# One operand of VectorE's two-input instructions, and the later modulation sums, moved to PSUM

## The chip, the core and the metric

The kernel runs on one core of one Trainium2 chip. The metric is the device time of one execution in microseconds (us); the figure for a kernel is the median of its runs. Engines are named as in the profile: PE is TensorE, DVE is VectorE, ACT is ScalarE, POOL is GpSimd, SP is the queue that issues the DMAs. SBUF is the large on-chip memory, PSUM the small one into which TensorE writes, here eight banks of 128 lanes by 512 float32.

## The reference

One block of a diffusion transformer with a hybrid mixer, batch 1, 512 tokens and 256 context tokens, width 2048. All is float32.

```python
mod = silu(c) @ w_mod + b_mod; mod_c = silu(c_ctx) @ w_mod + b_mod     # six chunks of 2048 each
h_lat = rms_norm(x, nw[0]) * (1 + sc_m) + sh_m                         # the context likewise
p = concat([h_ctx, h_lat]) @ w_in                                      # 6176 columns: x, y, q, k, v, z, gates
# RG-LRU, 8 heads of 128: conv of 4 taps over x, sigmoid gates r and i, then in both directions
log_a = -8 * r * softplus(-lam); a = exp(log_a); u = sqrt(-expm1(2 * log_a)) * (i * x)
h_t = a_t * h_{t-1} + u_t
lru = (h_forward + h_backward) * gelu(y)
# gated delta rule, 8 heads of 128, both directions: conv of 4 taps and silu over q, k, v; q, k l2-normalised;
# per chunk a unit lower triangular solve, then a recurrence of a 128x128 state over the chunks
gdn = rms_norm(o_forward + o_backward) * silu(z)
x = x + g_m * rms_norm(concat([lru, gdn]) @ w_out, nw[1])
h = rms_norm(x, nw[2]) * (1 + sc_f) + sh_f
out = x + g_f * rms_norm(square(relu(h @ w_ff1)) @ w_ff2, nw[3])
```

## The kernel before

Every large product runs in split form: an operand is cast to a high part (ScalarE, line 67, `wh<-wr`), the rest is a low part (a subtraction in `tt`, line 61, on VectorE or GpSimd, `wl<-wr,wh`), and three products high-high, high-low, low-high are summed in a bank.

The work falls in three stages. First the modulation chunks 0 and 1 are made for both streams (lines 308 to 332), and the context is normalised, scaled and shifted by `to_fm` (line 241). Second comes the mixer: `run_tiles` goes through a fixed list of tiles of 128 columns of `w_in`, each of 16 k-steps of three products (lines 498 to 500) into one bank; its order is the string `ORD`. A tile's evacuation (`lru_x`, `lru_y`, `Group.evac`, `z_evac`) begins when its last product has been issued. Third are the output projection in two passes of two token tiles (`project`, `prep`, `m_evac`), and then the squared-relu MLP (lines 1452 to 1465).

Between the tiles stands background work. Each piece is a Python generator (`Task`): a group of instructions, then a `yield` with its VectorE and ScalarE cost in us and the number of slots to let pass. `slot` is called after a quarter of a 512-token tile; it adds 2.8 us of VectorE budget and 2.2 us of ScalarE budget and lets tasks run while the budget holds. `boundary` ties each engine's instructions to within one to three slots of their place in the program. All of this is decided when the program is built. Engines run their instructions in program order, and an instruction that waits holds what is queued behind it on its engine.

What the change touches:

- `stt` (line 64) and `tt` (line 61) are the helpers through which nearly all two-input VectorE instructions go, so their rows carry these two lines and are told apart by tile names: `pg` is an SBUF page of 128x512, `bk` a bank, `macc` a running sum, `ld` a loaded page, `c` and `btL` are per-lane scalars.
- `bank()` takes one of eight banks from a single pool, for tiles and background work alike.
- `taps` (lines 509 to 511): three multiply-adds of a convolution, shifted by -2, -1 and +1. `Group.evac` (line 764 on) copies the tile out of its bank (775), scales it (776), runs the taps, a tanh (782), a product, and for the last of a pair transposes the result on TensorE (`transp`, 238).
- `lru_ctx` and `lru_lat` (lines 557 to 644): gates through tanh, then exp, tanh, sqrt on ScalarE and products and scans on VectorE.
- `Group.run`: decay masks (841 to 843), the inversion of 32x32 diagonal blocks on VectorE in 31 steps of a product and a subtraction (lines 893 to 900), block doubling by small products, then the recurrence over tiles, in which one step asks for up to five banks.
- `modacc` (line 1119): for each of the chunks 2 to 5 and each quarter of its columns, 16 loaded pages of `w_mod` are multiplied by a per-lane scalar and added up in `macc`, which is then stored in HBM. Chunks 2 to 4 run as a task from the mixer on; chunk 5 runs in the MLP, ordered behind `after`. GpSimd clears `macc` first (1123), and it has one buffer.

Of the kernel before, what the change touches and what calls it, by code (L numbers as in the profile page):

```python
# [7 lines left out]
F32 = mybir.dt.float32  # L8
# [8 lines left out]
P = 128  # L17
# [14 lines left out]
def build(tc, A, out, stop=None, dump=None):  # L32
# [3 lines left out]
    with es:  # L36
# [113 lines left out]
        # silu(c), silu(c_ctx)  # L150
# [12 lines left out]
        sm = es.enter_context(tc.tile_pool(name="small", bufs=4))  # L163

        def rsqrt(x, w):
            """x: [P, w] f32 (>0), returns tile with x^-0.5"""
            y = sm.tile([P, 16], I32, tag="rq_y", name=nm("rqy"))[:, :w]
            t = sm.tile([P, 16], F32, tag="rq_t", name=nm("rqt"))[:, :w]
            V.tensor_scalar(out=y, in0=x.bitcast(I32), scalar1=-0.5, scalar2=MAGIC, op0=ALU.mult, op1=ALU.add)
            yf = y.bitcast(F32)  # L170
            for _ in range(3):
                stt(t, yf, -0.5, yf, ALU.mult, ALU.mult)
                tt(V, t, t, x, ALU.mult)
                stt(yf, t, 1.5, yf, ALU.add, ALU.mult)
            return yf

        def softplus(dst, x, w):
            """dst = log(1+exp(x)); tiles [P, w]"""
# [5 lines left out]
            tt(V, e, q, m, ALU.add)                      # -|x|  # L184
# [3 lines left out]
            tt(V, e, e, q, ALU.mult)                     # s = e/(2+e)  # L188
            tt(V, q, e, e, ALU.mult)                     # s^2
# [8 lines left out]
        def rnorm(parts):  # L198
            """parts: 4 aps [P, 512] of one token tile -> 1/rms column"""
# [6 lines left out]
        def rfin(acc):  # L206
            """sums of squares of four parts -> 1/rms column; the guess is negative, each step flips the sign"""
# [33 lines left out]
        def to_fm(src, hi, lo, sc4, sh4):  # L241
            """token-major page -> (x*sc+sh) transposed, split into hi/lo views [P, 4, 128]"""
# [3 lines left out]
            tt(V, v4(x), v4(b), sc4.unsqueeze(2).to_broadcast(sh), ALU.mult)  # L246
            tt(V, v4(x), v4(x), sh4.unsqueeze(2).to_broadcast(sh), ALU.add)
# [24 lines left out]
        scol = const([P, 2, 16], F32, "scol")     # nw0*(1+sc)  (lat, ctx)  # L272
# [3 lines left out]
        def hctx(f):  # L276
            """one of hi, lo of the context's 4 feature tiles: two parts of two"""
# [56 lines left out]
        hgb = const([P, 4, 8], F32, "hgb")            # half gate biases, (dir,gate),head  # L334
# [5 lines left out]
        sp2 = const([P, 2, 8], F32, "sp2")             # 2*softplus(-lam)  # L340
        sp4 = const([P, 2, 8], F32, "sp4")             # -4*softplus(-lam)
# [8 lines left out]
        mpar = const([P, 2], F32, "mpar")              # lane's row parity (block, row parity, unit)  # L350
# [37 lines left out]
        def slot(part=1):  # L388
            """background work that goes with a quarter of a tile's products"""
# [127 lines left out]
        gateD = dp.tile([16, P, 512], F32, name="gateD")     # gelu gates, then silu gates  # L517

        def lru_x(h, n):
            """evacuation of one x tile: conv, then the recurrence as a task"""  # L520
            w = [cvw[:, j, h:h + 1] for j in range(4)]

            def evac(pt):
                xr = page()[:, :n]
                xc = page()[:, :n]
                if n == LAT:
                    S.copy(xc.rearrange("p (c r) -> p c r", r=8), pt.rearrange("p (r c) -> p c r", c=64))
                else:
                    S.copy(xc, pt[:, :n])
# [27 lines left out]
        def lru_ctx(h, xr):  # L557
# [3 lines left out]
            th = []  # L561
            for g in range(2):
                b = bank()
                t = page()
# [5 lines left out]
                th.append(t)  # L570
            yield 0, 1.5, 0
            tr, ti = th
# [5 lines left out]
            S.activation(tr, tr, AF.Sqrt)  # L578
            tv = ti.rearrange("p (d n) -> p d n", d=2)
            stt(tv, tv, 1.0, xr.unsqueeze(1).to_broadcast([P, 2, n]), ALU.add, ALU.mult)  # L580
            yield 0.6, 2.6, H0
            stt(tr, a, 1.0, tr, ALU.add, ALU.mult)
            stt(ti, tr, 0.5, ti, ALU.mult, ALU.mult)
            yield 1.3, 0, 0
            V.tensor_tensor_scan(ti[:, :n], a[:, :n], ti[:, :n], 0.0, ALU.mult, ALU.add)
            V.tensor_copy(lst[:, h, 0:1], ti[:, n - 1:n])
            u1, a1 = ti[:, n:], a[:, n:]
            V.tensor_tensor_scan(u1[:, ::-1], a1[:, ::-1], u1[:, ::-1], 0.0, ALU.mult, ALU.add)
# [4 lines left out]
        def lru_lat(h, xr):  # L593
# [3 lines left out]
            for d in range(2):  # L597
                for g, th in enumerate((tr, ti)):
# [3 lines left out]
                    S.activation(t, b, AF.Tanh, bias=hgb[:, 2 * d + g, h:h + 1], scale=0.5)  # L602
                    th.append(t)
                yield 0, 1.2, 0
# [7 lines left out]
            for d in range(2):  # L612
                S.activation(tr[d], tr[d], AF.Sqrt)
                stt(ti[d], ti[d], 1.0, xr, ALU.add, ALU.mult)
            yield 1.3, 1.1, H0
            for d in range(2):
                stt(tr[d], a[d], 1.0, tr[d], ALU.add, ALU.mult)
                stt(ti[d], tr[d], 0.5, ti[d], ALU.mult, ALU.mult)
                yield 1.3, 0, 0
            while h not in ldone:  # L620
                yield 0, 0, H0
            for d in range(2):
                init = lst[:, h, d:d + 1]
                u, v = ti[d], a[d]
                if d == 0:
                    V.tensor_tensor_scan(u, v, u, init, ALU.mult, ALU.add)
                else:
                    V.tensor_tensor_scan(u[:, ::-1], v[:, ::-1], u[:, ::-1], init, ALU.mult, ALU.add)
            res = ti
            del tr, a  # L630
# [4 lines left out]
            yield 1.4, 0, 0  # L635
            tt(V, res[0], res[0], res[1], ALU.add)
            yield 0.6, 0, H0
# [8 lines left out]
        def lru_y(h):  # L646
            def evac(py):
                x, t = page(), page()
                S.copy(x, py)
                S.activation(t, py, AF.Square)  # L650
# [898 lines left out]
```

## Time and profile before

| | |
|---|---|
| median of 3 runs | 2912.62 us |
| lowest, highest | 2910.87, 2915.26 us |
| span of the profiled execution | 2909.7 us |
| PE, DVE, ACT, POOL busy | 2664.2, 1877.2, 1230.1, 699.8 us |
| mean granted TensorE clock | 0.965 |

The profile is one execution. A group's row gives line, engine, operation, what it writes and reads, shapes, count, busy time and the mean of one in ns, then the idle time of the engine in front of it and what ended it. A row of the waits gives who waited, for what, the sum in us, the number of waits and the longest. A row of the timeline begins with the start in us and the duration in us. The stage rows give the busy time and count for each engine, the granted clock, the DMA share and GB/s. Matmuls overlap in TensorE's pipeline, so a busy TensorE is not always at its peak.

### The profile page before, as it was taken

The page shows a single profiled execution, that of the slowest core. Times are in us where ns is not written, and L with a number is a line of the kernel's source. Part 1 is how long each engine was busy: PE and PEld are TensorE (multiplying, and loading weights), DVE is VectorE, ACT ScalarE, POOL GpSimd, SP SyncE. Part 2 cuts the span into 40 slices and gives each one's busy share as a digit, 9 for nine tenths or more (in the row PEclk, how much of TensorE's full clock was granted, in tenths as well). Part 3 has the DMA queues.
Part 4 walks back from the last instruction along what each step waited for, and adds up shares of the span by engine and source line. Part 5 has one row for each costly group of instructions (what it writes and reads, how often), then busy time and mean ns, then how long its engine had stood idle before and what let it go on. Part 6 is the DMA issues. An engine that isn't in the chain of part 4 may idle for free.

```text
span 2909.7 us, 39480 instructions
## 1 busy us (share of the span) xinstructions
PE 2664.2 (92%) x14189; PEld 2187.2 (75%) x14189; DVE 1877.2 (65%) x3288; ACT 1230.1 (42%) x2438; POOL 699.8 (24%) x586
## 2 busy tenths in 40 slices
PE   5788898888988987996899999999999999999998
PEld 1277697677876876875689887888888888888886
DVE  6988868989898879774679644443344443344446
ACT  4546476564536654453454222222222222222223
POOL 3555345443435445332620000000000000000002
PEclk8899899999999998998999999999999999999999
DMA  7754365555655655764578733233332333332335
GB/s 263 259 161 120 103 172 151 148 158 164 191 164 178 188 166 165 232 201 159 183 243 267 235 101 116 94 101 95 96 100 94 97 99 95 100 96 95 101 94 156
DMA packets 376631, 436.41 MB, mean 150 GB/s; under 512 B 22793, under 2 KB 213602, under 8 KB 376434
## 3 DMA queue, kind: packets, MB, share of 16 engines
q1 hardware_dynamic: 376434, 433.89, 48.0%
q8 instruction: 111, 1.82, 0.3%
q14 instruction: 86, 0.70, 0.1%
HBM read 402.35 MB, written 31.46 MB: 149 GB/s over the span
## 4 chain that ended last, share of the span: by engine, by line
PE 49%; DVE 2%; DMA 1%; issue 0%; ACT 0%; POOL 0%; SPq 0%; DVEq 0%; ACTq 0%; POOLq 0%
PE bk L1465 8%; PE bk L1464 8%; PE bk L1463 8%; PE bk L1453 7%; PE bk L1454 7%; PE bk L1452 7%; PE bk L1375 1%; PE bk L1374 1%; PE bk L1373 1%; PE bk L1424 1%; PE bk L1423 1%; PE bk L1422 1%; DMA wr<-in_w_ff 1%; DVE pg L61 0%; DVE wl L61 0%
## 5 line engine op out<-in xcount | busy, mean ns | idle before, releaser
L67 ACT CAST wh<-wr 128x512 fp32r<-128x512 f32 x952 | 587.3, 619 | 1224.7 <-PE bk L1453 444.3
L61 DVE TENSOR_TENSOR wl<-wr,wh 128x512 fp32r<-128x512 f32 x642 | 457.3, 714 | 774.4 <-ACT wh L67 652.7
L61 POOL TENSOR_TENSOR wl<-wr,wh 128x512 fp32r<-128x512 f32 (+1 forms) x310 | 438.3, 1419 | 594.8 <-ACT wh L67 551.2
L1463 PE MATMUL bk<-wh,pg 128*128 128x512 f32 x960 | 373.5, 389 | 0.0
L1464 PE MATMUL bk<-wh,pg 128*128 128x512 f32 x960 | 373.5, 389 | 0.0
L1465 PE MATMUL bk<-wl,pg 128*128 128x512 f32 x960 | 373.4, 389 | 0.0
L1452 PE MATMUL bk<-H2h,wh 128*128 128x512 f32 x896 | 349.0, 389 | 0.0
L1454 PE MATMUL bk<-H2h,wl 128*128 128x512 f32 x896 | 348.6, 389 | 0.0
L1453 PE MATMUL bk<-H2l,wh 128*128 128x512 f32 x896 | 348.5, 389 | 0.0
L498 PE MATMUL bk<-Hlh,wh 128*128 128x512 f32 (+1 forms) x784 | 322.1, 411 | 2.8 <-ACT wh L67 2.8
L500 PE MATMUL bk<-Hlh,wl 128*128 128x512 f32 (+1 forms) x784 | 315.2, 402 | 5.4 <-POOL wl L61 5.4
L499 PE MATMUL bk<-Hll,wh 128*128 128x512 f32 (+1 forms) x784 | 314.7, 401 | 0.0
L61 POOL TENSOR_TENSOR big<-big,pg 128x512 f32<-128x512 f32 x9 | 12.0, 1343 | 1244.1 <-ACT pg L1525 1244.1
L64 DVE SCALAR_TENSOR_TENSOR macc<-ld,silc,macc 128x512 f32<-128x512 f32 x256 | 229.2, 895 | 20.5 <-DMA ld<-in_w_mod 13.1
L1463 PEld LDWEIGHTS bk<-wh,pg 128*128 128x128 f32 x960 | 180.2, 188 | 37.5
L1464 PEld LDWEIGHTS bk<-wh,pg 128*128 128x128 f32 x960 | 180.2, 188 | 37.3
L1465 PEld LDWEIGHTS bk<-wl,pg 128*128 128x128 f32 x960 | 180.2, 188 | 37.2
L1452 PEld LDWEIGHTS bk<-H2h,wh 128*128 128x128 f32 x896 | 168.2, 188 | 35.2 <-issue 0.2
L1453 PEld LDWEIGHTS bk<-H2l,wh 128*128 128x128 f32 x896 | 168.2, 188 | 35.1 <-issue 0.2
L1454 PEld LDWEIGHTS bk<-H2h,wl 128*128 128x128 f32 x896 | 168.2, 188 | 34.7
L500 PEld LDWEIGHTS bk<-Hlh,wl 128*128 128x128 f32 (+1 forms) x784 | 151.0, 193 | 43.4 <-POOL wl L61 8.9
L498 PEld LDWEIGHTS bk<-Hlh,wh 128*128 128x128 f32 (+1 forms) x784 | 151.8, 194 | 34.6 <-ACT wh L67 3.7
(335 smaller groups left out, 4756.6 us busy)
## 6 DMA issues: line engine op xcount, KB each, us to landing
wr<-in_w_ff SPq DMA_DIRECT2D x272, 512.0 KB, 3.6
wr<-in_w_in SPq DMA_DIRECT2D x144, 512.0 KB, 4.0
ld<-in_w_mod SPq DMA_DIRECT2D x256, 256.0 KB, 3.3
mr<-in_w_mod SPq DMA_DIRECT2D x32, 1024.0 KB, 5.3
wr<-in_w_out SPq DMA_DIRECT2D x64, 512.0 KB, 4.7
pg<-vkD SPq DMA_DIRECT2D x88, 128.0 KB, 3.8
ld<-in_x SPq DMA_DIRECT2D x32, 256.0 KB, 5.1
vkD<-pg SPq DMA_DIRECT2D x24, 256.0 KB, 2.1
```

What stands on the lines that cost most here:

```text
L61: e.tensor_tensor(out=out, in0=a, in1=b, op=op)
L64: V.scalar_tensor_tensor(out=out, in0=a, scalar=s, in1=b, op0=op0, op1=op1)
L67: S.copy(hi, src)
L498: T.matmul(pt[:m, :n], wh, a, start=k == 0, stop=False)
L499: T.matmul(pt[:m, :n], wh, b, start=False, stop=False)
L500: T.matmul(pt[:m, :n], wl, a, start=False, stop=k == 15)
L1452: T.matmul(bk[c], w[kk][0][:, s_], hh, start=k == 0, stop=False)
L1453: T.matmul(bk[c], w[kk][0][:, s_], hl_, start=False, stop=False)
L1454: T.matmul(bk[c], w[kk][1][:, s_], hh, start=False, stop=k == 15)
L1463: T.matmul(o, ah, h, start=k == 0, stop=False)
L1464: T.matmul(o, al, h, start=False, stop=False)
L1465: T.matmul(o, ah, l, start=False, stop=k == 3)
```

## The change

Wherever a two-input VectorE instruction of the mixer read both inputs from SBUF, one is now taken from a bank where that could be had: the product's own bank is read in place of a copy, ScalarE writes its result into a bank, or VectorE computes in a bank in place. Instructions stay on their engines but for a memset that goes from GpSimd to VectorE. The running sums of `modacc` live in a bank for chunks 2 to 4 (`after is None`) and are copied to SBUF by ScalarE at the end; for chunk 5 they stay. Declared costs of some `yield`s change with it. The weight splits (`wl<-wr,wh`), small square-root arithmetic and the splits of the first modulation rows are as before. Comments were taken out, which is not shown. The core of the diff:

```diff
 def to_fm(src, hi, lo, sc4, sh4):
-            tt(V, v4(x), v4(b), sc4.unsqueeze(2).to_broadcast(sh), ALU.mult)
-            tt(V, v4(x), v4(x), sh4.unsqueeze(2).to_broadcast(sh), ALU.add)
+            tt(V, v4(b), v4(b), sc4.unsqueeze(2).to_broadcast(sh), ALU.mult)
+            tt(V, v4(x), v4(b), sh4.unsqueeze(2).to_broadcast(sh), ALU.add)
 lru_x:
-                xc = page()[:, :n]
                 if n == LAT:
+                    xc = bank()
                     S.copy(xc.rearrange("p (c r) -> p c r", r=8), pt.rearrange("p (r c) -> p c r", c=64))
                 else:
-                    S.copy(xc, pt[:, :n])
+                    xc = pt[:, :n]
 lru_ctx (lru_lat in the same way):
+            stt(ti.rearrange("p (d n) -> p d n", d=2), b.rearrange("p (d n) -> p d n", d=2), 1.0,
+                xr.unsqueeze(1).to_broadcast([P, 2, n]), ALU.add, ALU.mult)
...
-            S.activation(tr, tr, AF.Sqrt)
-            stt(tv, tv, 1.0, xr.unsqueeze(1).to_broadcast([P, 2, n]), ALU.add, ALU.mult)
-            yield 0.6, 2.6, H0
-            stt(tr, a, 1.0, tr, ALU.add, ALU.mult)
-            stt(ti, tr, 0.5, ti, ALU.mult, ALU.mult)
+            u = bank()
+            S.activation(u, tr, AF.Sqrt)
+            yield 0, 2.6, H0
+            stt(u, a, 1.0, u, ALU.add, ALU.mult)
+            stt(u, u, 0.5, ti, ALU.mult, ALU.mult)
 lru_lat:
-                    V.tensor_tensor_scan(u, v, u, init, ALU.mult, ALU.add)
+                    V.tensor_tensor_scan(ti[0], a[0], u, init, ALU.mult, ALU.add)
 lru_y:
-                S.copy(x, py)
-                S.activation(t, py, AF.Square)
-                V.tensor_scalar(out=t, in0=t, scalar1=0.044715, scalar2=1.0, op0=ALU.mult, op1=ALU.add)
-                tt(V, t, t, x, ALU.mult)
+                S.activation(t, py, AF.Square, scale=math.sqrt(0.044715))
+                stt(t, t, 1.0, py, ALU.add, ALU.mult)
...
-                stt(t, t, 1.0, x, ALU.add, ALU.mult)
+                stt(t, t, 1.0, py, ALU.add, ALU.mult)
 Group.evac:
-                    raw = page()[:, :n]
-                    S.copy(raw, pt[:, :n])
+                    raw = pt[:, :n]
                     S.activation(dst, raw, AF.Copy, scale=w[2])
                     taps(dst, raw, w, n)
-                    yield 1.7, 1, 0
+                    yield 1.7, 0.6, 0
...
-                    th = page()
+                    th = bank()
                     S.activation(th, cv, AF.Tanh, scale=0.5)
                     stt(cv, th, 1.0, cv, ALU.add, ALU.mult)
 Group.run:
-                        S.activation(dt, bD, AF.Exp)
+                        S.activation(bD, bD, AF.Exp)
-                            stt(v4(dt)[:, u, :], v4(dt)[:, u, :], gt["bt"][:, o + u:o + u + 1], mk, ALU.mult, ALU.mult)
+                            stt(v4(dt)[:, u, :], v4(bD)[:, u, :], gt["bt"][:, o + u:o + u + 1], mk, ALU.mult, ALU.mult)
...
-                Wt = page(shape=(P, 16, 32))
+                wf = bank()
+                Wt = wf.rearrange("p (j i) -> p j i", i=32)
-                G.memset(Wt, 0.0)
+                V.memset(wf, 0.0)
...
-                    S.activation(oT, b, AF.Copy, scale=gnh)
+                    stt(oT, b, gnh, sz[p], ALU.mult, ALU.mult)
-                    tt(V, self.oT[p], self.oT[p], sz[p], ALU.mult)
 z_evac:
-                S.copy(x, pz)
-                stt(sz, sz, 1.0, x, ALU.add, ALU.mult)
+                stt(sz, sz, 1.0, pz, ALU.add, ALU.mult)
 modacc:
-            acc = page(tag="macc", bufs=1)
+            acc = seed = page(tag="macc", bufs=1)
             G.memset(acc, 0.0)
             SP.dma_start(acc[0:1, :], A["b_mod"][:, col:col + 512])
+            if after is None:
+                acc = bank()
-                    stt(acc, q.pop(0), silc[:, k - 1:k], acc, ALU.mult, ALU.add)
+                    stt(acc, q.pop(0), silc[:, k - 1:k], seed if k == 1 else acc, ALU.mult, ALU.add)
-            SP.dma_start(accD[4 * (chunk - 2) + f], acc)
+            if after is None:
+                S.copy(seed, acc)
+            SP.dma_start(accD[4 * (chunk - 2) + f], seed)
 m_evac:
-                    x = m1[t][c]
-                    tt(V, x, x, bk[t], ALU.add)
+                    tt(V, x, m1[t][c], x, ALU.add)
```

More of the change, by code (lines that the diff above doesn't have):

```diff
@@ L560, in lru_ctx @@
             yield 0, 0.9, 2 * H0
-            th = []
+            tr, ti = page(), page()
             for g in range(2):
                 b = bank()
-                t = page()
+                t = b if g else tr
                 for d in range(2):
@@ L577, in lru_ctx @@
                 S.activation(tr[:, sl], tr[:, sl], AF.Tanh, bias=sp2[:, d, h:h + 1], scale=sp2[:, d, h:h + 1])
-            S.activation(tr, tr, AF.Sqrt)
-            tv = ti.rearrange("p (d n) -> p d n", d=2)
-            stt(tv, tv, 1.0, xr.unsqueeze(1).to_broadcast([P, 2, n]), ALU.add, ALU.mult)
-            yield 0.6, 2.6, H0
-            stt(tr, a, 1.0, tr, ALU.add, ALU.mult)
-            stt(ti, tr, 0.5, ti, ALU.mult, ALU.mult)
+            u = bank()
[3 more added lines that the diff above has]
+            stt(u, u, 0.5, ti, ALU.mult, ALU.mult)
             yield 1.3, 0, 0
-            V.tensor_tensor_scan(ti[:, :n], a[:, :n], ti[:, :n], 0.0, ALU.mult, ALU.add)
+            V.tensor_tensor_scan(ti[:, :n], a[:, :n], u[:, :n], 0.0, ALU.mult, ALU.add)
             V.tensor_copy(lst[:, h, 0:1], ti[:, n - 1:n])
-            u1, a1 = ti[:, n:], a[:, n:]
-            V.tensor_tensor_scan(u1[:, ::-1], a1[:, ::-1], u1[:, ::-1], 0.0, ALU.mult, ALU.add)
+            u1, a1, s1 = ti[:, n:], a[:, n:], u[:, n:]
+            V.tensor_tensor_scan(u1[:, ::-1], a1[:, ::-1], s1[:, ::-1], 0.0, ALU.mult, ALU.add)
             V.tensor_copy(lst[:, h, 1:2], u1[:, 0:1])
@@ L597, in lru_lat @@
             for d in range(2):
-                for g, th in enumerate((tr, ti)):
+                for g in range(2):
                     b = bank()
@@ L601, in lru_lat @@
                     t = page()
-                    S.activation(t, b, AF.Tanh, bias=hgb[:, 2 * d + g, h:h + 1], scale=0.5)
-                    th.append(t)
-                yield 0, 1.2, 0
+                    S.activation(b if g else t, b, AF.Tanh, bias=hgb[:, 2 * d + g, h:h + 1], scale=0.5)
+                    (tr, ti)[g].append(t)
+                stt(ti[d], b, 1.0, xr, ALU.add, ALU.mult)
+                yield 0.7, 1.2, 0
             del gate
@@ L611, in lru_lat @@
             yield 0, 3, 0
[L612 to L619, printed above, removed]
             while h not in ldone:
                 yield 0, 0, H0
+            us = []
             for d in range(2):
+                u = bank()
+                S.activation(u, tr[d], AF.Sqrt)
+                us.append(u)
+            yield 0, 1.1, H0
+            for d in range(2):
+                u = us[d]
+                stt(u, a[d], 1.0, u, ALU.add, ALU.mult)
+                stt(u, u, 0.5, ti[d], ALU.mult, ALU.mult)
                 init = lst[:, h, d:d + 1]
-                u, v = ti[d], a[d]
                 if d == 0:
-                    V.tensor_tensor_scan(u, v, u, init, ALU.mult, ALU.add)
+                    V.tensor_tensor_scan(ti[0], a[0], u, init, ALU.mult, ALU.add)
                 else:
-                    V.tensor_tensor_scan(u[:, ::-1], v[:, ::-1], u[:, ::-1], init, ALU.mult, ALU.add)
+                    V.tensor_tensor_scan(u[:, ::-1], a[1][:, ::-1], u[:, ::-1], init, ALU.mult, ALU.add)
+                    tt(V, ti[0], ti[0], u, ALU.add)
+                yield 2.7 + 0.7 * d, 0, 0
             res = ti
-            del tr, a
+            del tr, a, us, u
             while h not in gy:
@@ L634, in lru_lat @@
             SP.dma_start(t, gateD[h])
-            yield 1.4, 0, 0
-            tt(V, res[0], res[0], res[1], ALU.add)
-            yield 0.6, 0, H0
+            yield 0, 0, H0
             pr = res[1]
@@ L647, in evac @@
             def evac(py):
-                x, t = page(), page()
-                S.copy(x, py)
-                S.activation(t, py, AF.Square)
-                V.tensor_scalar(out=t, in0=t, scalar1=0.044715, scalar2=1.0, op0=ALU.mult, op1=ALU.add)
-                tt(V, t, t, x, ALU.mult)
-                yield 1, 1, H0
+                t = page()
+                S.activation(t, py, AF.Square, scale=math.sqrt(0.044715))
+                stt(t, t, 1.0, py, ALU.add, ALU.mult)
+                yield 0.7, 0.6, H0
                 S.activation(t, t, AF.Tanh, scale=math.sqrt(2.0 / math.pi))
-                stt(t, t, 1.0, x, ALU.add, ALU.mult)
+                stt(t, t, 1.0, py, ALU.add, ALU.mult)
                 yield 0.6, 0.5, H0
@@ L1076, in run @@
                     oT = page()
-                    S.activation(oT, b, AF.Copy, scale=gnh)
+                    stt(oT, b, gnh, sz[p], ALU.mult, ALU.mult)
                     self.oT.append(oT)
-                yield 0, 1.2, H0
-                for p in range(2):
-                    tt(V, self.oT[p], self.oT[p], sz[p], ALU.mult)
                 del sz
-                yield 1.2, 0, 0
+                yield 1.4, 0, 0
                 for p in range(2):
@@ L1093, in f @@
             def f(pz):
-                x, sz = page(), page()
-                S.copy(x, pz)
+                sz = page()
                 S.activation(sz, pz, AF.Tanh, scale=0.5)
-                stt(sz, sz, 1.0, x, ALU.add, ALU.mult)
-                yield 0.6, 1, H0
+                stt(sz, sz, 1.0, pz, ALU.add, ALU.mult)
+                yield 0.7, 0.6, H0
                 SP.dma_start(gateD[8 + h], sz)
```

5 lines of the change are left out of this document (1 added, 4 removed).

## The prediction

> **What bounds the kernel now.** I read the page first, then the busy time by stage, then TensorE's waits in the stage that is not full, then a short piece of the timeline there, and last the groups of VectorE instructions.
>
> ```profile
> core 0: us, PE busy (x) PEld busy (x) DVE busy (x) ACT busy (x) POOL busy (x), PEclk, DMA share, GB/s
> 0.00:146.00 146.00, 97.69 (x345) 33.35 (x345) 115.69 (x201) 77.84 (x105) 66.63 (x57) 0.87 0.78 260
> 146.00:1455.00 1309.00, 1130.62 (x7160) 952.61 (x7160) 1052.80 (x1946) 710.82 (x1572) 591.68 (x497) 0.94 0.56 167
> ...
> 1600.00:2850.00 1250.00, 1247.33 (x5496) 1031.52 (x5495) 548.78 (x842) 348.68 (x572) 1.05 (x2) 1.00 0.34 107
> ```
>
> From 1600 us on TensorE is busy 1247 of 1250 us at the full clock: nothing that VectorE does there can move the end, and the change touches next to nothing in it. The first 146 us are loads and the splits of the first modulation rows, which stay as they are. The mixer and the output projection, 146 to 1455 us, are the stage to look at: TensorE is idle for 1309 - 1131 = 178 us of it, at a clock of 0.94, while VectorE is busy 1052.8 us, 80%. TensorE's waits there, with what ended them, are the following (engine, tile and line that waited, what ended it, us in total, times, longest):
>
> ```profile
> PE bk L238 <- DVE pg L64: 56.1, 14, 8.7
> PE bk L500 <- DVE wl L61: 19.9, 8, 3.8
> PE bk L928 <- DVE pg L904: 18.4, 4, 8.8
> PE bk L238 <- DVE pg L61: 11.0, 5, 6.3
> PE bk L1373 <- ACT pg L67: 10.2, 3, 5.4
> PE bk L1373 <- ACT M L67: 7.3, 1, 7.3
> PE bk L500 <- POOL wl L61: 6.7, 9, 1.7
> PE bk L1375 <- POOL wl L61: 5.8, 5, 2.3
> ```
>
> VectorE ended 56.1 + 19.9 + 18.4 + 11.0 = 105.4 us of them, GpSimd 12.5. L238 is the transpose of a page that VectorE has just finished; TensorE runs in program order, so when VectorE is late the weight products queued behind that transpose stand too. None of these waits is for the evacuation of a bank: all are for inputs.
>
> Why VectorE is late shows in front of the longest of them, 8.7 us, whose transpose waits for the last row here, done at 501.86 us. Three VectorE instructions ahead of it, and what GpSimd and ScalarE do beside them:
>
> ```profile
> 487.17 1.80 DVE L64 SCALAR_TENSOR_TENSOR pg<-pg,pg 128x512 f32<-128x512 f32 x1
> 488.89 1.78 DVE L64 SCALAR_TENSOR_TENSOR macc<-ld,silc,macc 128x512 f32<-128x512 f32 x1
> 490.60 1.77 DVE L64 SCALAR_TENSOR_TENSOR pg<-pg,pg 128x512 f32<-128x512 f32 x1
> ...
> 501.17 0.69 DVE L64 SCALAR_TENSOR_TENSOR pg<-pg,pg 128x512 f32<-128x512 f32 x1 [2.04 <-ACT pg L782]
> ```
>
> ```profile
> 487.13 4.69 POOL L61 TENSOR_TENSOR wl<-wr,wh 128x512 fp32r<-128x512 f32 x3 [5.87 <-ACT wh L67]
> ```
>
> ```profile
> 499.21 1.28 ACT L782 ACT_TABLE_LOAD   x1 [9.89 <-DVE pg L64]
> ```
>
> Three GpSimd splits in 4.69 us and three VectorE instructions of 1.8 us interleave: the two engines take turns, one instruction each. ScalarE's queue then stands 9.89 us for VectorE. The groups say that this is general, and which instructions it spares. Contended, in this stage (count, busy us, mean ns):
>
> ```profile
> L64 DVE SCALAR_TENSOR_TENSOR macc<-ld,silc,macc 128x512 f32<-128x512 f32 x192 | 181.3, 944 | 12.4 <-DMA ld<-in_w_mod 6.7 <-DMA macc<-in_b_mod 3.8
> L64 DVE SCALAR_TENSOR_TENSOR pg<-pg,c,pg 128x510 f32<-128x510 f32 (+1 forms) x168 | 137.7, 819 | 9.0 <-DMA wr<-in_w_in 3.3 <-ACT pg L776 3.0 <-ACT pg L530 0.6
> L64 DVE SCALAR_TENSOR_TENSOR pg<-pg,pg 128x512 f32<-128x512 f32 x120 | 101.6, 854 | 50.0 <-ACT pg L578 18.1 <-ACT pg L782 15.0 <-ACT pg L613 8.6
> L61 DVE TENSOR_TENSOR pg<-pg,L 128x126 f32<-128x126 f32 (+22 forms) x186 | 84.2, 453 | 4.4
> ...
> L61 DVE TENSOR_TENSOR pg<-pg,pg 128x126 f32<-128x126 f32 (+23 forms) x202 | 77.5, 384 | 5.1
> L64 DVE SCALAR_TENSOR_TENSOR pg<-bk,exL,pg 128x128 f32<-128x128 f32 x64 | 19.0, 342 | 1.1 <-ACT pg L1048 1.0
> L61 DVE TENSOR_TENSOR pg<-pg,shc 128x512 f32<-128x512 f32 x18 | 18.5, 1041 | 0.0
> ...
> L64 DVE SCALAR_TENSOR_TENSOR pg<-pg,btL,LE 128x128 f32<-128x128 f32 x32 | 17.4, 603 | 7.9 <-ACT pg L841 7.9
> ...
> L61 DVE TENSOR_TENSOR pg<-bk,scol 128x512 f32<-128x512 f32 x18 | 12.0, 680 | 0.2 <-PE bk L238 0.2
> ```
>
> And from 1560 to 1900 us, where GpSimd has nearly nothing to do:
>
> ```profile
> L61 DVE TENSOR_TENSOR wl<-wr,wh 128x512 fp32r<-128x512 f32 x131 | 90.1, 689 | 138.3 <-ACT wh L67 109.6 <-PE bk L1464 20.3 <-PE bk L1453 6.1
> L64 DVE SCALAR_TENSOR_TENSOR macc<-ld,silc,macc 128x512 f32<-128x512 f32 x53 | 39.7, 749 | 7.0 <-DMA ld<-in_w_mod 5.3 <-DMA macc<-in_b_mod 0.7
> ```
>
> The same running sum takes 944 ns beside GpSimd and 749 ns without it. With one operand from a bank (pg<-bk) the contended stage has 680 ns at 512 columns and 342 ns at 128: no dearer than two SBUF operands alone (689), and untouched by GpSimd. The lines scol and shc are neighbours in one function, 680 against 1041 ns.
>
> **The change, part by part.** Each contended group loses its excess over the row with a bank operand.
> Running sums, chunks 2 to 4: 192 x (944 - 749) = 37.4 us. Chunk 5 keeps its SBUF sum, and has no GpSimd beside it.
> Convolution taps, now reading the product's bank: 96 of about 511 columns and 72 of about 255. Their price alone lies on the line through 342 ns at 128 and 749 ns at 512 columns, both with a scalar per lane: 748 and 477 ns, 106.1 us for the 168, so 137.7 - 106.1 = 31.6 us.
> The 120 pg<-pg,pg (silu, gelu, recurrence inputs): 120 x (854 - 680) = 20.9 us.
> Shift adds: 18 x (1041 - 680) = 6.5 us, and the 8 of the MLP's input at the same price 2.9 us.
> Decay masks: 32 x (603 - 342) = 8.4 us, and there are 96 of them in the code: 25 us.
> The 32x32 inversion, 31 steps of two for six groups: no row shows it alone. The sums lose 21% and the taps 23%, so I take 22% of 84.2 + 77.5 us = 35.6 us; the bounds are nothing and the masks' 43%, 70 us.
> Scans keep their bounds from the same shares and aren't counted. The gelu loses one VectorE instruction of three, the group's memset comes over from GpSimd; these are eight and six instructions and cancel.
> Sum: 37.4 + 31.6 + 20.9 + 9.4 + 25 + 35.6 = 160 us, so VectorE's load falls from 1052.8 to 893 of 1309 us, 80.4% to 68.2%.
>
> Writing a bank from VectorE or ScalarE stands nowhere in this trace. [...]
> [...]
>
> The relief is no gain by itself: it lies beside TensorE's work. It counts where TensorE waits for VectorE. Work queued in front of a waiting step grows with load over spare time: 80.4/19.6 = 4.1 before, 68.2/31.8 = 2.1 after, about half. In the example the three instructions lose 1.80 - 0.68, 1.78 - 0.75 and 1.77 - 0.68 = 3.2 of 8.7 us, 37%, before counting what stood in front of them. I take 55%, as turns between the engines bunch just where both are loaded: 0.55 x 105.4 = 58 us. Bounds: VectorE's relief share, 160/1053 = 15% or 16 us, and the whole 105 us.
> GpSimd is freed of the same turns; of its 12.5 us I take half, 6 us.
>
> ```profile
> L775 ACT COPY pg<-bk 128x512 f32<-128x512 f32 x24 | 14.0, 582 | 0.0
> ```
>
> The copies out of the banks go. They stand at the head of the chain copy, scale, taps, tanh, product, transpose: 14 waits x 0.58 = 8 us, if none is hidden; nothing otherwise.
>
> ```profile
> L498 PE MATMUL bk<-Hlh,wh 128*128 128x512 f32 x768 | 315.1, 410 | 2.8 <-ACT wh L67 2.8
> L500 PE MATMUL bk<-Hlh,wl 128*128 128x512 f32 x768 | 308.2, 401 | 5.4 <-POOL wl L61 5.4
> L499 PE MATMUL bk<-Hll,wh 128*128 128x512 f32 x768 | 307.8, 401 | 0.0
> ```
>
> ```profile
> L1463 PE MATMUL bk<-wh,pg 128*128 128x512 f32 x960 | 373.5, 389 | 0.0
> ```
>
> These products take 410, 401 and 401 ns where the clock is 0.94 and 389 ns where it is 1.00: 768 x (21 + 12 + 12) = 34.6 us. The lower clock goes with the idle stretches; with (58 + 6 + 8)/178 = 40% of the idle time gone I take 40% of it, 14 us; none to all.
>
> Added work: one ScalarE copy for each of the twelve sums, ahead of the store that GpSimd's next memset waits for, with GpSimd's splits queued behind it. At 0.58 us that is 7 us if all is exposed, and more if the copy stands behind a wait in ScalarE's queue. I cost it at nothing: the 12.5 us of waits on splits are all that TensorE feels of GpSimd now.
> The recurrence's square roots move behind the wait for the context's last state, and its add moves up; both stay inside their task. No DMA is moved or added.
>
> Total 58 + 6 + 8 + 14 = 86 us off the profiled execution, whose span is
>
> ```profile
> span 2909.7 us, 39480 instructions
> ```
>
> and the median of the runs, 2912.6 us, is 2.9 us above it: 2909.7 - 86 + 2.9 = 2827 us.
>
> **Rivals.** *ScalarE is next.* The long waits end in a serial chain with a tanh and its table load, and 9.89 us of ScalarE's standing shows how tightly the two are coupled. If the chain's length and not VectorE's backlog sets the wait, each of the 14 loses only a copy, three taps at 0.15 us and one product at 0.17 us, 1.2 us: 17 us, with 6 of GpSimd and 5 of clock 28 us, 2885 us. For it: in the example VectorE stood 2.04 us for the tanh before the product. Against: ScalarE had stood 9.89 us for VectorE's late taps before that.
>
> *Banks run out, and it is slower.* The mixer's banks now also hold a running sum through sixteen steps, the inversion's matrix through 31, two recurrence inputs, and each product tile until its taps are done, out of eight; a recurrence step over the tiles asks for five more. If TensorE has to wait for a release, it waits about a slot, 2.8 us by the rate in the code. Two such waits in each of the 24 recurrence steps are 134 us, 48 more than the gain: 2961 us. It decides from 86/2.8 = 31 waits on. Against: no wait of the list is for a bank now, so several stand free at most times.
> [...]
>
> *It does not do what it says.* If the turns were about writing SBUF, or the pointer scalar, a bank operand would spare nothing and the time would stay at 2913 us. The rows with a bank, an SBUF page and a pointer scalar at 342 ns speak against it.
>
> **How the numbers follow.** The forecast's mechanism with a gain of 50 to 145 us gets 0.66; more than that 0.03; the ScalarE rival 0.18; banks 0.08; nothing happening 0.05. The range runs from 2770 us, where nearly all of VectorE's waits and the clock are won (143 us), to 2890 us, just past the ScalarE rival; it leaves out banks, no effect, the extremes. A measurement here tells 0.2%, about 6 us, from no change. Faster is 0.66 + 0.03 + 0.18 = 0.87, with 0.06 for same and 0.07 for slower, a little of the banks' case ending even.
>
> **What would show it.** Right: the sums of chunks 2 to 4 near 749 ns, the taps near 748 and 477, masks at 342; VectorE near 890 us busy in the mixer; L238's waits on VectorE about halved; the clock above 0.94. Wrong: those durations unchanged, or new VectorE rows with a bank as output 60 ns dearer; L238's waits passing to ScalarE; a wait in front of a tile's first product that an evacuation ended.

## The result, and the profile after

The changed kernel takes 2834.89 us, the median of 4 runs (2833.44 to 2838.08), beside 2913.94 us for 4 runs of the kernel before: a ratio of 0.9725, 95% interval 0.9713 to 0.9738, or 79 us. The forecast was 2827 us. The profiled execution has a span of 2836.3 us, 73.4 us less than before.

First the busy time by stage after the change; the columns are those of the prediction's first view.

```profile
core 0: us, PE busy (x) PEld busy (x) DVE busy (x) ACT busy (x) POOL busy (x), PEclk, DMA share, GB/s
...
146.00:1380.00 1234.00, 1119.70 (x7157) 950.40 (x7155) 880.38 (x1946) 674.69 (x1510) 527.94 (x490) 0.95 0.59 176
...
1520.00:2770.00 1250.00, 1247.31 (x5489) 1031.50 (x5488) 548.72 (x844) 346.38 (x570) 1.05 (x2) 1.00 0.34 107
```

The stage with the mixer is chosen to hold the same work as before: 7157 matmuls against 7160, and 1946 VectorE instructions in both. It lasts 1234 us in place of 1309, and that is the whole result; the MLP is the same. TensorE's idle time there went from 178 to 1234.0 - 1119.7 = 114 us, 64 us less, and its busy time from 1130.6 to 1119.7, 11 us less. VectorE's busy time fell by 172 us, so 172 - 75 = 97 us of what VectorE was spared, more than half, bought nothing.

TensorE's waits in this stage after the change (who waited, for what, us, times, longest):

```profile
PE bk L238 <- DVE pg L64: 18.3, 6, 5.6
PE bk L925 <- DVE pg L901: 12.0, 4, 9.4
PE bk L238 <- DVE pg L61: 11.0, 3, 6.3
PE bk L1369 <- ACT pg L67: 10.7, 2, 6.7
PE bk L500 <- POOL wl L61: 8.9, 9, 1.8
PE bk L1012 <- DVE pg L64: 7.5, 4, 4.3
...
PE bk L238 <- DVE pg L228: 4.2, 1, 4.2
...
PE bk L500 <- DVE wl L61: 3.8, 4, 1.3
PE bk L238 <- DVE bk L887: 3.7, 1, 3.7
PE bk L552 <- DVE pg L61: 2.7, 1, 2.7
PE bk L552 <- DVE pg L64: 2.3, 1, 2.3
PE bk L1371 <- POOL wl L61: 1.3, 1, 1.3
```

Line numbers moved a little: 925 was 928, 1369 was 1373, 1371 was 1375. The four rows on VectorE that the prediction added up to 105.4 us are now 18.3 + 12.0 + 11.0 + 3.8 = 45.1 us. The transposes gave most of it, 56.1 to 18.3 us, and the low parts 19.9 to 3.8. The two rows on GpSimd went from 12.5 to 10.2 us. But neither list is the whole. Added up over all rows of the two views, and not only those printed, TensorE's waits on VectorE are 122.5 us before and 74.5 after, on GpSimd 24.9 and 16.6, on ScalarE 27.0 and 22.7, on DMAs 3.5 and none: 177.9 and 113.8 us, which is the idle time. So VectorE was worth 48 us and not the 60 of the four rows, since other waits on it grew or came up: L671, L1012, the transposes behind L228 and L887, and L552.

VectorE's groups in the same stage:

```profile
L64 DVE SCALAR_TENSOR_TENSOR bk<-ld,silc,bk 128x512 f32<-128x512 f32 x180 | 134.5, 747 | 9.4 <-DMA ld<-in_w_mod 7.5
L64 DVE SCALAR_TENSOR_TENSOR pg<-bk,c,pg 128x510 f32<-128x510 f32 (+1 forms) x168 | 105.8, 630 | 42.4 <-ACT pg L773 31.0 <-ACT pg L530 9.2
L61 DVE TENSOR_TENSOR wl<-wr,wh 128x512 fp32r<-128x512 f32 (+1 forms) x112 | 96.0, 858 | 107.1 <-ACT wh L67 100.1 <-PE bk L1371 4.3 <-ACT pg L67 2.6
L61 DVE TENSOR_TENSOR pg<-bk,L 128x126 f32<-128x126 f32 (+22 forms) x186 | 58.8, 316 | 4.5
L61 DVE TENSOR_TENSOR bk<-bk,pg 128x126 f32<-128x126 f32 (+22 forms) x186 | 48.4, 260 | 5.0
L64 DVE SCALAR_TENSOR_TENSOR pg<-bk,pg 128x512 f32<-128x512 f32 x56 | 38.3, 687 | 30.0 <-ACT bk L779 14.4 <-ACT bk L601 8.1 <-ACT bk L568 7.4
...
L64 DVE SCALAR_TENSOR_TENSOR bk<-bk,pg 128x512 f32<-128x512 f32 x24 | 16.5, 692 | 0.3
...
L64 DVE SCALAR_TENSOR_TENSOR bk<-ld,silc,macc 128x512 f32<-128x512 f32 x12 | 12.1, 1006 | 26.0 <-DMA macc<-in_b_mod 18.4 <-issue 5.5 <-POOL wl L61 1.5
L61 DVE TENSOR_TENSOR pg<-bk,shc 128x512 f32<-128x512 f32 x18 | 12.0, 681 | 0.1
...
L64 DVE SCALAR_TENSOR_TENSOR pg<-bk,btL,LE 128x128 f32<-128x128 f32 x32 | 9.0, 343 | 19.7 <-ACT bk L838 19.7
```

The running sums are at 747 ns where they were at 944, the taps at 630 (819), the products of the inversion at 316 (453), the shift adds at 681 (1041), the masks at 343 (603). The third row is the check on this: VectorE's own low parts still read two SBUF pages, and their price did not fall, 858 ns where 103 of them took 814. The row of twelve stands out: the first step of each of the twelve sums still reads two SBUF pages, at 1006 ns, and VectorE stands 26.0 us in front of these twelve, where it stood 12.4 us in front of all 192 before. Idle time in front of the taps also grew, 9.0 to 42.4 us, 31.0 of it for ScalarE's scaling (L773, once L776 with 3.0 us); no run shows why.

The two engines beside each other, at a busy place a little after the prediction's example (start, duration):

```profile
506.89 1.29 POOL L61 TENSOR_TENSOR wl<-wr,wh 128x512 fp32r<-128x512 f32 x1 [1.16 <-ACT wh L67]
508.15 0.73 POOL L61 TENSOR_TENSOR pg<-pg,pg 128x256 fp32r<-128x256 f32 x1
508.85 1.29 POOL L61 TENSOR_TENSOR wl<-wr,wh 128x512 fp32r<-128x512 f32 x1
```

```profile
507.74 0.69 DVE L64 SCALAR_TENSOR_TENSOR bk<-pg,bk 128x512 f32<-128x512 f32 x1
508.46 0.70 DVE L64 SCALAR_TENSOR_TENSOR bk<-bk,pg 128x512 f32<-128x512 f32 x1
509.07 0.74 DVE L64 SCALAR_TENSOR_TENSOR pg<-bk,c,pg 128x510 f32<-128x510 f32 x1
```

GpSimd works without a break from 506.89 to 510.14 us, and three VectorE instructions begin and end inside at 0.69 to 0.74 us each; in the prediction's example such instructions took 1.77 to 1.80 us. GpSimd gains too, 1.29 us for a split where three took 4.69.

### The profile page after: what moved, and what is told of

Same layout as the page of the kernel before. It is cut to its first block, busy times and chain, and to the rows that moved or that the text cites. A ratio compares the mean times of both kernels' runs of the same rounds, so it can differ in the third digit from the quotient of the medians.

```text
span 2836.3 us, 39412 instructions
## 1 busy us (share of the span) xinstructions
PE 2652.2 (94%) x14189; PEld 2187.4 (77%) x14189; DVE 1694.6 (60%) x3286; ACT 1193.2 (42%) x2374; POOL 639.1 (23%) x580
## 4 chain that ended last, share of the span: by engine, by line
PE 57%; DVE 3%; DMA 2%; issue 1%; POOL 1%; ACT 1%; SPq 0%; DVEq 0%; ACTq 0%; POOLq 0%
PE bk L1461 8%; PE bk L1459 8%; PE bk L1460 8%; PE bk L1448 7%; PE bk L1450 7%; PE bk L1449 7%; PE bk L1370 2%; PE bk L1371 2%; PE bk L1369 2%; PE bk L1420 1%; PE bk L1419 1%; PE bk L1418 1%; DVE pg L61 1%; DMA wr<-in_w_ff 1%; PE bk L498 1%
## 5 line engine op out<-in xcount | busy, mean ns | idle before, releaser
L61 POOL TENSOR_TENSOR wl<-wr,wh 128x512 fp32r<-128x512 f32 (+1 forms) x310 | 403.8, 1308 | 594.5 <-ACT wh L67 537.2
L498 PE MATMUL bk<-Hlh,wh 128*128 128x512 f32 (+1 forms) x784 | 318.5, 406 | 0.0
L61 POOL TENSOR_TENSOR big<-big,pg 128x512 f32<-128x512 f32 x9 | 12.2, 1369 | 1248.0 <-ACT pg L1521 1248.0
L1461 PEld LDWEIGHTS bk<-wl,pg 128*128 128x128 f32 x960 | 180.3, 188 | 37.6 <-DVE wl L61 0.4
L1460 PEld LDWEIGHTS bk<-wh,pg 128*128 128x128 f32 x960 | 180.3, 188 | 37.4
L498 PEld LDWEIGHTS bk<-Hlh,wh 128*128 128x128 f32 (+1 forms) x784 | 150.0, 191 | 31.0 <-ACT pg L1045 0.2
L499 PEld LDWEIGHTS bk<-Hll,wh 128*128 128x128 f32 (+1 forms) x784 | 150.0, 191 | 30.4
```

Of the source, the lines that this page charges most:

```text
L61: e.tensor_tensor(out=out, in0=a, in1=b, op=op)
L498: T.matmul(pt[:m, :n], wh, a, start=k == 0, stop=False)
L499: T.matmul(pt[:m, :n], wh, b, start=False, stop=False)
L1460: T.matmul(o, al, h, start=False, stop=False)
L1461: T.matmul(o, ah, l, start=False, stop=k == 3)
```

## Experiments

Ratios are to the kernel before on the same chip. The changed kernel has 0.9725. Kernels that ran on different chips are compared by these ratios, and a difference of two ratios carries both intervals.

**The running sums alone, and everything but them.** The first kernel puts these lines into the `modacc` of the kernel before, the second takes them out of the changed kernel.

```diff
+            if after is None:
+                acc = bank()
...
-stt(acc, q.pop(0), silc[:, k - 1:k], acc, ...)
+stt(acc, q.pop(0), silc[:, k - 1:k], seed if k == 1 else acc, ...)
...
+            if after is None:
+                S.copy(seed, acc)
```

> The kernel before, with only the running sums of chunks 2 to 4 in a bank. Turns theory (VectorE and GpSimd exclude each other where a VectorE instruction has two SBUF inputs, and TensorE waits for the backlog): the sums go from 944 to about 749 ns, 37 us of VectorE relief; the whole change turned 172 us of relief into 79 us of time, 0.46 for each, so about 17 us less, near 2896 us, ratio 0.994. Copies theory (the gain is the ScalarE copies that went from the head of each evacuation): no copy goes here, one is added per sum, so no gain, ratio 1.000.

> The changed kernel with the running sums of chunks 2 to 4 back in SBUF, all else as changed. Turns theory: sums back to 850 to 940 ns, 17 us more than the changed kernel, near 2852 us, ratio to before 0.979. Copies theory: as the changed kernel, 2835 us, ratio 0.9725. Banks theory (a bank held through sixteen steps costs TensorE something): faster than the changed kernel, under 2835 us.

The sums alone: 2905.89 us (10 runs), 0.9970 (0.9959 to 0.9981), 9 us. The changed kernel without them: 2851.83 us (4 runs), 0.9784 (0.9771 to 0.9798), 17 us slower than with them. Each sum's step has its price as forecast, 748 ns in the first kernel and 944 in the second. So the same relief of VectorE is worth 9 us alone and 17 us on top of the rest. The first is half of what was expected, 17 us, and the second is as expected. In the first kernel VectorE again stands in front of the first steps:

```profile
L64 DVE SCALAR_TENSOR_TENSOR bk<-ld,silc,macc 128x512 f32<-128x512 f32 x12 | 11.3, 941 | 22.2 <-DMA macc<-in_b_mod 13.1 <-POOL M L61 3.5 <-DMA wr<-in_w_in 3.2
```

The sum's end is now a copy on ScalarE, a store, GpSimd's clear of the one page, and a load of the first row, and the next sum's first step waits for all four with VectorE's whole queue behind it. All but the copy were there before the change. The second kernel has the chain without the copy, and its waits for that load are 9.8 us, between the 3.8 of the kernel before and the 18.4 of the changed kernel:

```profile
L64 DVE SCALAR_TENSOR_TENSOR macc<-ld,silc,macc 128x512 f32<-128x512 f32 x192 | 181.3, 944 | 20.5 <-DMA macc<-in_b_mod 9.8 <-DMA ld<-in_w_mod 8.7
```

**The copies out of the banks put back.** All 72 copies by ScalarE are made again, now into a bank, so that VectorE's operands stay in PSUM; the declared costs follow.

```diff
-                    raw = pt[:, :n]
+                    raw = bank()[:, :n]
+                    S.copy(raw, pt[:, :n])
```

> The changed kernel, but the ScalarE copies stay and put the tile into a second bank, from which VectorE reads (72 copies: conv inputs of the mixer's groups and of the context's x tiles, gelu and silu gates, the normalised output). VectorE's operand still comes from a bank. Turns theory: the operand decides, so within 10 us of the changed kernel, 2835 to 2845 us, ratio 0.973 to 0.977. Copies theory: most of the gain is given back, 2880 us or more, ratio 0.988 or more.

2851.71 us (4 runs), 0.9787 (0.9774 to 0.9800): 17 us slower, which neither theory expected (at most 10 us, or 45 and more). The copies cost about twice the 8 us of the prediction, and are the smaller part of the gain. VectorE's steps keep their prices there, 748 ns for a sum. Each copy put back also takes one more bank, and ScalarE's time from what waits behind it: TensorE's waits on ScalarE, over all rows, are 30.7 us beside 22.7, and the transposes' row on VectorE 28.8 beside 18.3. How the 17 us divide was not separated.

**The inversion's matrix alone in a bank.**

```diff
-                Wt = page(shape=(P, 16, 32))
+                wf = bank()
+                Wt = wf.rearrange("p (j i) -> p j i", i=32)
...
-                G.memset(Wt, 0.0)
+                V.memset(wf, 0.0)
```

> The kernel before, with only the matrix of the 32x32 inversion in a bank, cleared by VectorE. Turns theory: its 372 products and subtractions lose about 45 us of VectorE time together, at 0.46 for each 21 us less, near 2892 us, ratio 0.993. Copies theory: no copy goes, ratio 1.000. If relief counts only where a transpose waits for VectorE soon after (18 of PE's 105 us of waits on VectorE follow an inversion), less: about 10 us, ratio 0.9965.

2889.70 us (4 runs), 0.9916 (0.9904 to 0.9929), 24 us, as expected (21 us). VectorE's busy time over the whole run falls by 37.6 us here and by 38.7 us with the sums alone, and yet the first is worth 24 us and the second 9: how much of a relief counts depends on where it falls. Its 372 steps take as long as in the changed kernel:

```profile
L61 DVE TENSOR_TENSOR pg<-bk,L 128x126 f32<-128x126 f32 (+22 forms) x186 | 58.4, 314 | 4.2
L61 DVE TENSOR_TENSOR bk<-bk,pg 128x126 f32<-128x126 f32 (+22 forms) x186 | 48.7, 262 | 4.6
```

**No SBUF reads by GpSimd's weight splits, before and after.** Each split on GpSimd is replaced by two clears of the same page. The low parts of these weights are zeros then, and the clears no longer wait for ScalarE's cast, so the chain cast, split, product is shorter too.

```diff
-                split(r, h, l, eng[c % 2])
+                if eng[c % 2] is G:
+                    S.copy(h, r)
+                    G.memset(l.bitcast(F32), 0.0)
+                    G.memset(l.bitcast(F32), 0.0)
+                else:
+                    split(r, h, l, eng[c % 2])
```

> The kernel before, but GpSimd's weight splits are left out: in place of each subtraction GpSimd clears the low part twice (two memsets, about 1.05 us in place of 1.44), so it works about as long but reads no SBUF. VectorE and PSUM use are as before. Turns theory: VectorE's two-input instructions lose their excess without any bank operand (sums near 749 ns, taps near 630), and most of the whole change's gain comes without the change: 2815 to 2850 us, ratio 0.966 to 0.979. Copies theory, or any in which PSUM itself is what helps: 2900 us or more, since nothing of the change is in it.

> The changed kernel with the same left out: GpSimd clears the low parts of its weight splits twice and reads no SBUF for them. Turns theory: few turns are left to lose (the splits on VectorE, the small square-root arithmetic, some masks' inputs), 40 us of VectorE relief at 0.46 and earlier splits: 2810 to 2825 us, ratio 0.965 to 0.970; against the kernel before with the same edit it keeps only what the copies were worth, 10 to 25 us. If the change gained by something else than turns, the two stay 60 us or more apart.

The kernel before: 2766.73 us (4 runs), 0.9476 (0.9449 to 0.9504). The changed one: 2793.22 us (4 runs), 0.9562 (0.9538 to 0.9586). Both are faster than expected, the first by 48 us at least and the second by 17, and the shorter chain may be some of that, so these times are no measure of the turns alone; the prices are. In the kernel before, with its operands all in SBUF:

```profile
L64 DVE SCALAR_TENSOR_TENSOR macc<-ld,silc,macc 128x512 f32<-128x512 f32 x213 | 163.3, 767 | 14.8 <-DMA ld<-in_w_mod 8.5 <-DMA macc<-in_b_mod 4.4
L64 DVE SCALAR_TENSOR_TENSOR pg<-pg,c,pg 128x510 f32<-128x510 f32 (+1 forms) x168 | 113.4, 675 | 16.9 <-ACT pg L781 8.6 <-ACT pg L535 6.2
```

```profile
L475 POOL MEMSET wl<- 128x512 f32 x303 | 159.9, 528 | 16.4
```

VectorE's prices fall from 944 to 767 (21 of these 213 sums belong to chunk 5) and from 819 to 675 ns though GpSimd writes as many bytes twice over: GpSimd's reads make the turns, not its writes. That shows the cause of the relief, with no operand moved. The second finding was not forecast: without the splits' reads the order is reversed, and the changed kernel is 26.5 us slower than the kernel before. Apart from the turns, the change costs something. The next experiments look for it.

**Fewer banks.** The pool has seven banks in the changed kernel, as shown, and six in the kernel before.

```diff
-        pg = ps = es.enter_context(tc.tile_pool(name="psum", bufs=8, space=PSUM))
+        pg = ps = es.enter_context(tc.tile_pool(name="psum", bufs=7, space=PSUM))
```

> The changed kernel with seven banks in place of eight. Banks theory (the held banks are near the limit): TensorE waits for releases, 20 us or more lost, 2855 us or more, ratio 0.980 or more. If banks stand free at most times, within 6 us of the changed kernel, 2829 to 2841 us.

> The kernel before with six banks in place of eight. If banks stand free in it, as the absence of waits for a release in its list says: within 6 us of 2913 us, ratio 0.998 to 1.002. If it needs them, slower by 10 us or more.

The changed kernel with seven: 2854.93 us (4 runs), 0.9777 (0.9754 to 0.9800), 15 us more by the ratios; on this chip the kernel before takes 2919.59 us. The kernel before with six: 2927.01 us (10 runs), 1.0024 (1.0012 to 1.0035), 7 us more. Both lie between the two answers that were expected, nearer to the one that banks are short for the changed kernel and nearer to the one that they are not for the kernel before. TensorE's waits with seven banks have these rows:

```profile
PE bk L552 <- DVE pg L64: 10.4, 3, 7.2
...
PE bk L498 <- DVE pg L64: 8.4, 3, 5.1
...
PE bk L552 <- DVE pg L61: 3.4, 1, 3.4
```

L498 holds a tile's first product and L552 a gate's. Their inputs come from ScalarE and GpSimd, so a wait there on VectorE is taken here for one on the last reader of the bank that is to be written; the profile does not name the bank. The three rows are 22.2 us with seven banks. The changed kernel with its eight has 2.7 + 2.3 = 5.0 us at L552 and none at L498 on VectorE, and the kernel before has no such row. So the banks are close to their limit. In the changed kernel without GpSimd's reads these waits are 0.9 us: they do not explain the 26.5 us.

**The seed page ahead.** The page from which a sum starts is cleared and loaded eight steps before the sum begins, and the finished sum is copied into a page of its own.

```diff
+                if k == 8 and after is None and (chunk, f) < (4, 3):
+                    mkseed(chunk + (f + 1) // 4, (f + 1) % 4)
...
             if after is None:
+                seed = page()
                 S.copy(seed, acc)
```

> The changed kernel, but the page from which a running sum starts is cleared and filled with its row eight steps before the sum begins, and a finished sum is copied into a page of its own; the sums still run in a bank. Seed theory: VectorE, which stood 26.0 us in front of the twelve first steps (before: 12.4 us in front of all 192 steps), loses that stand, the waits of TensorE on VectorE's late pages shrink by some of it, and the time falls from 0.9725 of the kernel before to 0.963 to 0.969, 2806 to 2823 us. Rival, banks and order: the stands in front of the first steps go to below 5 us and the time stays within 6 us of 2835, since VectorE, 68% busy, has spare time elsewhere for them.

> The same with GpSimd's weight splits replaced by two clears that read no SBUF, and their low parts left out of the products, as in the two earlier kernels that did so (before 0.9476, changed 0.9562 of the kernel before). No turns are left to win here, so the gap of 27 us between those two is what the change costs apart from the turns. Seed theory: most of the gap goes, ratio 0.947 to 0.951, 2762 to 2773 us. Rival, longer undivided groups in the gated recurrence or bank holding: ratio 0.954 to 0.957, 2783 to 2792 us.

The first: 2824.24 us (4 runs), 0.9680 (0.9661 to 0.9700), 13 us less than the change as it stands, and the fastest here of the kernels that compute the whole block. The stand has gone:

```profile
L64 DVE SCALAR_TENSOR_TENSOR bk<-ld,silc,macc 128x512 f32<-128x512 f32 x12 | 12.5, 1041 | 0.8 <-DMA ld<-in_w_mod 0.8
```

Without the splits' reads (low parts left out as above) it gives nothing: 2794.69 us (4 runs), 0.9569 (0.9546 to 0.9593), though the stand, 21.1 us there, fell to 0.0. So the seed chain is a real cost of the changed kernel, 13 us of time for the 26.0 us of standing, and it is not what the kernel without the reads loses. The 13 us are for the whole chain, of which the change added the copy.

**The gated recurrence as before.** The edit put back both halves of it, `lru_ctx` and `lru_lat`; the expectation names only the first.

```diff
-            u = bank()
-            S.activation(u, tr, AF.Sqrt)
+            S.activation(tr, tr, AF.Sqrt)
...
-            yield 0, 2.6, H0
-            stt(u, a, 1.0, u, ALU.add, ALU.mult)
+            yield 0.6, 2.6, H0
+            stt(tr, a, 1.0, tr, ALU.add, ALU.mult)
```

> The changed kernel without the SBUF reads of GpSimd's weight splits, with the context half of the gated recurrence (lru_ctx) as in the kernel before: its products back between SBUF pages, its square root and add in their old order and its group cut in two again. Theory of the longer undivided groups: half or more of the 27 us goes, ratio 0.947 to 0.952, 2762 to 2776 us. Rivals, seed or bank holding: no change from 0.9562, 2785 to 2792 us.

2797.46 us (5 runs), 0.9584 (0.9565 to 0.9603), beside 0.9562: no gain. The theory of the longer groups falls, for both halves.

**The order of before.** The seed page ahead, and every declared cost and cut between groups as before the change, with the operands kept in banks but for the latent scans and adds.

```diff
-                    yield 1.7, 0.6, 0
+                    yield 1.7, 1, 0
...
-                stt(u, u, 0.5, ti[d], ALU.mult, ALU.mult)
+                stt(ti[d], u, 0.5, ti[d], ALU.mult, ALU.mult)
+                yield 1.3, 0, 0
```

> The changed kernel with its seed page ahead (0.968 of the kernel before), and with the declared costs and the cuts between groups as before the change, so that TensorE's instructions stand in exactly the order of the kernel before; in the changed kernel up to 104 small products stand earlier or later against the weight products. The operands stay in banks, but for the sixteen scans of the latent half and its eight adds, which go back to SBUF pages, some 8 us more of VectorE's work. Order theory: the 27 us that the change costs apart from the turns are pieces of work that now stand side by side in the program and wait for each other; most of it comes back, 0.958 to 0.962 of the kernel before, 2796 to 2808 us. Rival, the places themselves (banks held, ScalarE writing banks, chains without their copies): no gain, 0.966 to 0.971, 2819 to 2834 us. If the order of before is itself tuned to the stalls that the turns make, slower than 0.971.

2828.51 us (5 runs), 0.9686 (0.9668 to 0.9704): no gain over 0.9680. The order theory falls too, with one reservation: the scans that went back to SBUF cost VectorE some 8 us, which could hide a few us.

## Why the prediction was right, point by point

- **The stage and the bound.** Only the mixer's stage changed, by 75 us, as argued from the full MLP.
- **VectorE's relief.** Forecast 160 us, measured 172. By groups: sums 34.7 (37.4 forecast; the twelve first steps stayed at 1006 ns), taps 31.9 (31.6), all 96 masks 23.4 (25). For the inversion the prediction's rows held 16 adds of 512 columns that belong elsewhere, 12.0 us; without them it fell from 149.7 to 107.2 us, 42.5 (35.6). It was the term most mis-sized: with instructions of 16 to 136 columns its products lost 30% and not 22%. Scans, not counted, fell by 13.8 us, those of 512 columns from about 1780 to 1275 ns.
- **The price of a bank.** The forecast's sum holds nothing for writing a bank, and no run shows a price: VectorE's instruction that reads and writes banks takes 692 ns beside 687 for one that writes a page, and ScalarE's tanh in front of the group's product takes 601 ns into a bank (L779) where it took 631 ns into a page (L782). The 60 ns in the prediction's list of signs rest on no run either. As a source a bank costs nothing that shows: 681 to 692 ns in the rows above with a bank as one source, 689 with two SBUF pages and GpSimd silent.
- **TensorE's waits on VectorE.** Forecast 58 us less. The four rows that it was worked out from lost 60, but VectorE's waits over all rows 48, 39% of 122.5: the prediction read its list as the whole, and waits came up in rows that it did not hold. The share of 55% stood on a choice between 15% and the whole, so its nearness to the four rows is in part luck. The prediction's law for it, load over spare time, does not hold for the parts: by it the first relief is worth the most, and the sums bought 9 us alone and 17 after the rest.
- **GpSimd's waits.** Forecast 6 us; the two rows it took lost 2.3, all rows 8.3. That 12.5 us are all that TensorE feels of GpSimd was a misreading: it is 24.9 us, with the gates' splits and the masks' pages. The weight splits did become faster, as the rows before and after show, 1436 to 1323 ns, but they wait for ScalarE's cast, which ended most of GpSimd's idle time in both.

```profile
L61 POOL TENSOR_TENSOR wl<-wr,wh 128x512 fp32r<-128x512 f32 x304 | 435.1, 1436 | 585.8 <-ACT wh L67 542.1 <-PE bk L1015 8.2 <-DMA pg<-vkD 6.5
```

```profile
L61 POOL TENSOR_TENSOR wl<-wr,wh 128x512 fp32r<-128x512 f32 x304 | 400.7, 1323 | 587.6 <-ACT wh L67 530.4 <-PE bk L1031 17.4 <-PE bk L499 8.8
```

- **The clock.** Forecast 14 us on the long products, measured 768 x (4 + 3 + 4) ns = 8.4 us, from 410, 401 and 401 ns to these:

```profile
L498 PE MATMUL bk<-Hlh,wh 128*128 128x512 f32 x768 | 312.1, 406 | 0.0
L499 PE MATMUL bk<-Hll,wh 128*128 128x512 f32 x768 | 305.6, 398 | 0.0
L500 PE MATMUL bk<-Hlh,wl 128*128 128x512 f32 x768 | 305.1, 397 | 1.8 <-POOL wl L61 1.8
```

The idle time fell by 36%, and 8.4 of the 34.6 us came back, a quarter, so taking the clock in proportion was too much. TensorE's whole busy time in the stage fell by 11 us. By the clock that the traces record, TensorE ran at half speed in 26 stretches of this stage before, 160 us in all, and in 24 after, 123 us: fewer idle us, but nearly as many slow stretches.

- **The copies.** Forecast 8 us; putting all 72 back cost 17, with the reservation made there. The prediction looked at the 24 copies of one row; the others also went from ScalarE's queue.
- **Added work, costed at nothing.** This is the step that failed, if a small one. The copy at a sum's end lengthened the chain copy, store, clear, load in front of the next first step. The prediction asked what GpSimd has queued behind it and saw no one wait; it did not ask what VectorE has behind the first step. VectorE stood 26.0 us there, and with the page made ahead 13 us of the time came back. Not all of it is the copy's: the waits for the load are 3.8 us before, 9.8 us with everything but the sums changed, and 18.4 us with them.
- **The sum.** Forecast 86 us, of which 72 were idle time of TensorE and 14 its busy time; the stage gave 64 and 11, and the median of the runs 79. The mechanism came as forecast; that the total came within 7 us owes something to errors that cancel, VectorE's waits and the copies 18 us too large together (66 for 48) and GpSimd's 2 too small, with ScalarE's (4) and the DMAs' (3.5) not counted. With the seed page ahead the gain is 93 us (0.9680).
- **The rivals.** ScalarE next: VectorE does stand for it more, 236 us in the stage where it was 170, but TensorE's waits on ScalarE fell, 27.0 to 22.7 us, and the gain is far above this rival's 28 us; it fell. Does nothing: fell, and the kernels without the splits' reads show the turns themselves. Banks run out: its price did not come, 5.0 us of waits and not 134, but it was near; one bank less costs 15 us.
- **What stays open.** Without GpSimd's reads the changed kernel is 26.5 us slower than the kernel before. The seed chain, the cuts of the gated recurrence and TensorE's waits for banks are ruled out there; the order was tried only with the reads in place, and gave nothing. In those two kernels, the changed one first, TensorE's waits on VectorE are 61 and 40 us over all rows, and VectorE's idle time for ScalarE 258 and 211 us in the 23 largest rows of each. That points to chains between these two engines, for example in front of the taps:

```profile
L64 DVE SCALAR_TENSOR_TENSOR pg<-bk,c,pg 128x510 f32<-128x510 f32 (+1 forms) x168 | 105.9, 630 | 46.1 <-ACT pg L778 32.6 <-ACT pg L535 11.3
```

The first tap stands 32.6 us for ScalarE's scaling there, and 8.6 us (L781) in the row of its counterpart, quoted with those two kernels. Which part of the change lengthens them was not separated, and the cause stays open.

## What to carry to other kernels

Where VectorE and GpSimd take turns in reading SBUF, look for the group's price where the other engine is silent and for a neighbour with one operand in PSUM: the difference of those rows is what the engine can be spared. How much of that reaches the end has to be read from the waits, all rows of them: here 79 of 172 us did, and for two parts of 38 us each it was 9 and 24. Count the banks held as a resource before and after, since one bank decided 15 us here. And of each accumulator that moves, follow its start and its end, with the queue behind its first step, as closely as its many steps in between.

## What the runs showed of the hardware

- Here VectorE and GpSimd took turns for GpSimd's reads, not for its writes: with two clears of 528 ns in the place of each split, the sums took 767 ns (944 beside splits).
- One operand in a bank was enough for VectorE to be spared (747 ns for ld and a bank, 749 for two SBUF pages with GpSimd silent), and GpSimd was spared in turn, 1436 to 1323 ns; a bank as VectorE's output cost nothing that shows, 692 against 687 ns.
- TensorE's clock fell to half in stretches, and their number hardly followed the sum of the idle time: 26 stretches, 160 us, at 178 us idle, and 24, 123 us, at 114.
